# A hybrid decoder layer: three kinds of stores on another queue, rotation tables in two steps, gate weights one unit sooner

## The chip, the cores and the metric

The kernel runs on one core of a Trainium2 chip. A core has a matrix engine (TensorE, PE in the rows; its weight loads are PEld), a vector engine (VectorE, DVE), a scalar engine (ScalarE, ACT), a general one (GpSimd, POOL) and SyncE (SP), which here only starts transfers. Each engine takes its own instructions strictly in order. A transfer (DMA) is started by an instruction on an engine's queue and is then carried out by 16 DMA engines beside the compute; in this kernel nearly all are started from SP, a few from ACT. The metric is the device time of one execution in microseconds, the median of three runs. The granted clock in the rows is 1.00 when TensorE has its full 2.4 GHz and 0.50 at 1.2 GHz; a row between the two is a mean over a stretch.

## The reference

One layer on 2048 tokens of width 1024, all in float32:

```python
h = rmsnorm(x, norm_w)
u, z_s, q, k, v, z_a = split(h @ w_in, 6)            # six blocks of 512 columns
# group A: 32 groups of 16 channels, each a 64-dim complex diagonal state space
xr, xi = associative_scan(a, B u)                      # over 2048 positions
y = gelu(Re(C x) + D * u)
y_s = y * sigmoid(y @ glu_w + glu_b) * silu(z_s)
# group B: 4 heads, two query/key maps of 64, value of 128, causal
q, k = rope(rmsnorm(q)), rope(rmsnorm(k))
w = softmax(q0 k0') - lam * softmax(q1 k1')
y_a = rmsnorm(w @ v) * (1 - lambda_init) * silu(z_a)
x = x + concat(y_s, y_a) @ w_out
gate = sigmoid(x @ ple_w_gate)                         # 1024 x 1024
x = x + gate * (p @ ple_w_proj)                        # p has 256 columns
```

## The kernel before

Every float32 product is made as three passes on TensorE: each operand is split into a high part (a copy rounded to TensorE's float type, made on ACT) and a low part (the rest, made on DVE or POOL by a subtraction), and high x high, high x low and low x high are summed. Intermediate results go to DRAM tensors whose names end in `_scr` and are read back.

**Projections and state space (0 to about 700 us).** The loop at L736 runs over 12 blocks (a half of the tokens, one of the six column blocks), and in each over 4 units of 256 tokens. Eight weight tiles `wraw` of a block are loaded on SP (L279) and split on ACT (L282, `wh`) and DVE (L283, `wl`); a ring of 8 split tiles (`WB`) means that the next block's tiles are made while the last unit of the block runs. Values are scaled on ACT and stored (L831, L832), queries and keys are normalised, rotated, transposed, split and stored as high and low parts (L871, L872). Beside that runs the generator `ssm()` in steps, as background work: for each of 32 channel groups, `ahead` loads the group's input `U` and its rotation table `tab`, TensorE makes two products, DVE rotates by the table, scans and rotates back, and `behind` copies the result to `ysb` on ACT and stores it to `yg_scr` (L652, L653). For every four groups `four` makes what the next four need, in steps of which one is taken per group: it loads parameters, makes `na`, then products and the split `wa`, then two rotation tables `tx` of 128 x 544 on DVE (L581 to L585), each stored to `tab_scr` (L586); `tx` has one buffer, so that the second table is begun when the first one's store has landed. At the end the state-space results pass the half-GLU.

**Attention (about 700 to 1158 us).** Four heads, each over query blocks of 256; the output projection's first half (`pmf`, L928) runs beside it.

**Output projection's second half and the gate (from about 1122 us).** The loop at L1176 takes eight units t = 0 to 7 of 256 tokens. A unit loads `x1` and the attention results, multiplies by `w_out` (L928: in PSUM tile `pmf` for t below 3, `EOP`, in `pm` after that) and adds to `x1` on DVE (L1185, L1189). Between units the gate's weights are prepared: the gate product is made in a way that needs seven combinations of the quarters of `w_gate`, and the generator `gate_w` (L1142) makes their splits in four blocks k = 0 to 3, two steps (`yield`) each. A block loads two 512 KB pieces `wgr` (L1161) in the only two buffers; ahead of each load POOL copies one element of `last[0]`, the `x1` of the unit that was finished one unit earlier, into the buffer (L1160), which holds the load back until that unit's sum is there. ACT makes the high parts (L1149), DVE the differences (L1154) and low parts (L1150), POOL the other low parts (L1150). `GWS` says after which unit how many of the eight steps are written: 2 after t = 3 and t = 4, 3 after t = 5, 1 after t = 6. After the loop `operands` splits the finished `x1` (ACT L1235 `oph`, POOL L1236 `opl`), in memory that the pools of the gate preparation give back, `ple_w` loads the last projection's weights through one buffer `pi` (L1212), and TensorE makes the gate products (L1262) and the last projection (L1278).

**What sets the order.** The program is written in a language with tiles and pools; a scheduler orders each engine's instructions when the program is built, by their priorities (the written order, with background work put behind by `LAG` and attention's scores ahead by `SADV`) and a simulation of its own. A change in one place can thus shuffle instructions elsewhere.

Of the kernel before, what the change touches and what calls it, by code (L numbers as in the profile page):

```python
# [11 lines left out]
F32 = mybir.dt.float32  # L12
# [3 lines left out]
ALU = mybir.AluOpType  # L16
# [49 lines left out]
WB = 8  # L66
ACB = 3
EOP = 3
GWS = {3: 2, 4: 2, 5: 3, 6: 1}
XEB = 14  # L70
RA3 = 2
SSE = 0
# [46 lines left out]
def hymba_kernel(ctx, tc, x_t, p_t, positions, norm_w, w_in, lam_re, lam_im, log_dt, b_re, b_im,  # L119
                 c_re, c_im, ssm_d, glu_w, glu_b, q_norm_w, k_norm_w, lq1, lk1, lq2, lk2,  # L120
                 subln_w, w_out, w_proj, w_gate, out):
    nc = tc.nc
    V, A, G, T = nc.vector, nc.scalar, nc.gpsimd, nc.tensor
# [74 lines left out]
    with ExitStack() as p1:  # L198
# [114 lines left out]
        def ssm():  # L313
# [198 lines left out]
            with tc.tile_pool(name="ssB", bufs=2) as sp:  # L512
# [3 lines left out]
                def split(x_, nm, cols):  # L516

                    hi = sp.tile([128, cols], F32R, name=nm + "h", bufs=SPB[nm])
                    lo = sp.tile([128, cols], F32R, name=nm + "l", bufs=SPB[nm])
                    h_, l_ = hi, lo  # L520
                    if len(x_.shape) > 2:
                        g_, k_, p_ = x_.shape[1:]
                        h_, l_ = (t_.rearrange("q (g l p) -> q g l p", g=g_, l=k_) for t_ in (hi, lo))
                    A.copy(h_, x_)
                    V.tensor_tensor(l_, x_, h_.bitcast(F32), op=ALU.subtract)
                    return hi, lo
# [7 lines left out]
                def spread(par4, o_, l0):  # L534

                    r_ = sp.tile(sh, F32, name="na", bufs=1)
                    t_ = sp.tile([128, 2, 17, 16], F32, name="tabt", bufs=1).rearrange("q s a b -> q (s a b)")[:, :512]
                    t_ = t_.rearrange("q (g l p) -> q g l p", g=4, l=L)
                    V.tensor_tensor(r_, par4[:, :, o_:o_ + 16].unsqueeze(2).to_broadcast(sh),
                                    par4[:, :, 65 + l0:73 + l0].unsqueeze(3).to_broadcast(sh), op=ALU.mult)  # L540
                    V.tensor_tensor(t_, par4[:, :, o_ + 16:o_ + 32].unsqueeze(2).to_broadcast(sh),
                                    par4[:, :, 74 + l0:82 + l0].unsqueeze(3).to_broadcast(sh), op=ALU.mult)
                    V.tensor_tensor(r_, r_, t_, op=ALU.add)
                    return r_

                def four(q4, out_):


                    par4 = sp.tile([128, 4, NPAR], F32, name="parg")
                    nc.sync.dma_start(par4, par_scr[q4])  # L550
                    pt2 = sp.tile([128, 2, NTAB], F32, name="pt2", bufs=1)
                    nc.sync.dma_start(pt2, ptab_scr[q4])
                    na = spread(par4, 0, 1)

                    dd = sp.tile([128, 4, GP], F32, name="dd")
                    nc.sync.dma_start(dd.rearrange("q g p -> q (g p)"), ssm_d[0, q4 * 64:q4 * 64 + 64].partition_broadcast(128))
                    G.affine_select(out=dd, in_=dd, pattern=[[0, 4], [-1, GP]], compare_op=ALU.is_equal,
                                    fill=0.0, base=-112, channel_multiplier=1)
                    yield
                    pr_ = ps_ss.tile([128, 512], F32, name="pss")  # L560
                    for g in range(4):
                        T.matmul(pr_[:, g * 16:g * 16 + 16], lhsT=na[:, g].rearrange("q l p -> q (l p)"),
                                 rhs=par4[:, g, 32:48], start=True, stop=True)
                    rs = sp.tile([128, 64], F32, name="rs", bufs=1)
                    V.tensor_tensor(rs, pr_[:, :64], dd.rearrange("q g p -> q (g p)"), op=ALU.add)
                    nc.sync.dma_start(r_scr[q4][0:128, :], rs)
                    M = sp.tile([128, L, 64], F32, name="M", bufs=1)

                    r0 = r_scr[q4][0:128, :]
                    nc.sync.dma_start(M, bass.AP(tensor=r0.tensor, offset=r0.offset, ap=[[64, 128], [GP * 64, L], [1, 64]]))  # L570
                    pw_ = ps_ss.tile([128, 512], F32, name="pss")
                    for g in range(4):
                        T.transpose(pw_[:, g * 128:g * 128 + 128], na[:, g].rearrange("q l p -> q (l p)"), ident)
                    wa = split(pw_, "wa", 512)
                    yield

                    sht = [128, 2, 17, 16]
                    for e in range(2):
                        tx = sp.tile(sht, F32, name="tx", bufs=1)
                        t1 = sp.tile(sht, F32, name="tabt", bufs=1)  # L580
                        V.tensor_tensor(tx, pt2[:, e, 0:17].unsqueeze(1).unsqueeze(3).to_broadcast(sht),  # L581
                                        pt2[:, e, 34:66].rearrange("q (s b) -> q s b", s=2).unsqueeze(2).to_broadcast(sht), op=ALU.mult)
                        V.tensor_tensor(t1, pt2[:, e, 17:34].unsqueeze(1).unsqueeze(3).to_broadcast(sht),
                                        pt2[:, e, 66:98].rearrange("q (s b) -> q s b", s=2).unsqueeze(2).to_broadcast(sht), op=ALU.mult)
                        V.tensor_tensor(tx, tx, t1, op=ALU.add)  # L585
                        nc.sync.dma_start(tab_scr[q4 * 2 + e], tx)  # L586
                    yield
                    wc = spread(par4, 32, 0)
                    out_[q4] = par4, wa, M, wc
                    yield  # L590
# [21 lines left out]
                for g in range(NG):  # L612
# [35 lines left out]
                    def behind(g=g, py=py, w=[w_[:, gs] for w_ in wc4], xa=xa):  # L648

                        product(py, w, xa, first=False)  # L650
                        ysb = sp.tile([128, NCH], F32, name="ysb", bufs=YSB)
                        A.copy(ysb, py)  # L652
                        nc.sync.dma_start(yg_scr[g].rearrange("l p c -> (l p) c"), ysb)  # L653
                        if g % 8 == 7:
                            for l in range(L):
                                nc.sync.dma_start(
                                    y_scr[(g - 7) * GP:(g + 1) * GP, l, :].rearrange("(g p) c -> g p c", p=GP), yg_scr[g - 7:g + 1, 7 - l])
# [78 lines left out]
        for bi, (hf, kind, c0) in enumerate(blocks):  # L736
            leaving = bi == len(blocks) - 1 or blocks[bi + 1][0] != hf
            for t in range(4):
# [75 lines left out]
                else:  # L814
# [3 lines left out]
                    for j in range(2):  # L818
# [10 lines left out]
                        if kind == "v":  # L829
                            vo = pt.tile([128, 512], F32, name="t2")  # L830
                            A.activation(vo, pm, AF.Copy, scale=rstd[:, ti:ti + 1])  # L831
                            nc.sync.dma_start(v_scr[rows, :], vo)  # L832
                        elif kind == "za":
                            zz = pt.tile([128, 512], F32, name="t2")
                            A.activation(zz, pm, AF.Copy, scale=rstd[:, ti:ti + 1])
# [32 lines left out]
                            V.scalar_tensor_tensor(sl_[dst], ptr, nrm[kind][2], sh_[dst].bitcast(F32), op0=ALU.mult, op1=ALU.subtract)  # L868
                    if kind in ("q", "k"):
                        hi_s, lo_s = (qh_scr, ql_scr) if kind == "q" else (kh_scr, kl_scr)  # L870
                        nc.sync.dma_start(hi_s[:, :, tok:tok + 256].rearrange("h q t -> q h t"), sh_.bitcast(F32))  # L871
                        nc.sync.dma_start(lo_s[:, :, tok:tok + 256].rearrange("h q t -> q h t"), sl_.bitcast(F32))  # L872
                if kind == "u" and (bi, t) != (1, 3):
                    squares(xseq[xi + t])
# [521 lines left out]
```

## Time and profile before

| | us |
|---|---|
| median of three runs | 1471.44 (1465.84 to 1471.6) |
| the profiled execution, whole | 1468.54 |
| its span, first to last instruction | 1466.8 |
| PE busy | 1389.2 (95%) |
| DVE busy | 1067.0 (73%) |
| ACT busy | 768.0 (52%) |
| POOL busy | 522.4 (36%) |

PE is busy or nearly so all along, so the time is the time of TensorE's passes and what it idles. The idle times are read stretch by stretch and by what ended them. A busy PE does not say that it works at its peak, since passes overlap; where the peak matters, the rows below give passes per stretch.

### The profile page before, as it was taken

How to read it: one execution, taken by the hardware profiler on the slowest of the kernel's cores; microseconds unless marked ns; L12 is line 12 of the kernel's file. 1: busy time of each engine (PE TensorE's matmuls, PEld its weight loads, DVE VectorE, ACT ScalarE, POOL GpSimd, SP SyncE). 2: the span in 40 equal slices, each digit the busy share in tenths (PEclk: the TensorE clock that was granted, in tenths of full speed). 3: DMA queues.
4: the chain of work that ended last, by engine and by line, in shares of the span. 5: the costliest groups of instructions: out<-in, count | busy, mean ns of one | idle time of the engine just before them, and what ended most of it. 6: DMA issues, size and time to landing. Idle time of an engine off the chain costs nothing.

```text
span 1466.8 us, 27419 instructions
## 1 busy us (share of the span) xinstructions
PE 1389.2 (95%) x9602; PEld 1279.5 (87%) x9602; DVE 1067.0 (73%) x2527; ACT 768.0 (52%) x1689; POOL 522.4 (36%) x670
## 2 busy tenths in 40 slices
PE   7999899999899999999899999999999996999998
PEld 7998798778698878888699999988989896899998
DVE  8568788789898866774687767767887248656754
ACT  8543335456554545553577677777787213332231
POOL 6632410043010411340255455544335334543440
PEclk9999899999999999999999999999999998899999
DMA  7448666546755287556854644644443455132221
GB/s 244 131 127 263 200 190 210 159 125 211 237 179 177 94 232 185 150 168 203 255 145 125 181 127 119 177 127 152 116 144 122 153 189 205 58 116 76 70 80 58
DMA packets 219410, 230.34 MB, mean 157 GB/s; under 512 B 62712, under 2 KB 168328, under 8 KB 216712
## 3 DMA queue, kind: packets, MB, share of 16 engines
q1 hardware_dynamic: 216968, 224.40, 49.8%
q10 hardware_dynamic: 2304, 4.20, 0.8%
q8 instruction: 75, 1.23, 0.3%
q14 instruction: 63, 0.52, 0.1%
HBM read 152.19 MB, written 84.72 MB: 162 GB/s over the span
## 4 chain that ended last, share of the span: by engine, by line
PE 48%; DVE 19%; DMA 15%; ACT 6%; issue 6%; POOL 5%; SPq 2%; ACTq 0%; DVEq 0%; POOLq 0%
PE pg L1262 11%; PE pmf L928 7%; PE po L1099 7%; PE pss L1063 7%; PE ptw L1095 3%; PE pl L1278 3%; DMA wraw<-in_w_in_dram 3%; PE pmm L824 2%; PE pss L707 2%; PE pmm L778 2%; POOL qst L846 2%; DMA tab_scr<-tx 2%; DVE wl L283 2%; PE pm L928 2%; DVE zz L644 1%
## 5 line engine op out<-in xcount | busy, mean ns | idle before, releaser
L824 PE MATMUL pmm<-wh,xh 128*128 128x512 f32 x512 | 197.6, 395 | 7.0 <-ACT wh L282 6.6
L824 PE MATMUL pmm<-wl,xh 128*128 128x512 f32 x512 | 200.8, 395 | 2.1 <-DVE wl L283 2.1
L824 PE MATMUL pmm<-wh,xl 128*128 128x512 f32 x512 | 200.2, 393 | 0.0
L1063 PE MATMUL pss<-ks,qd 128*128 128x512 f32 (+3 forms) x640 | 185.1, 387 | 7.5 <-DVE st L1065 4.0
L1074 ACT ACTIVATE s<-s,st 128x1024 f32<-128x1024 f32 (+4 forms) x192 | 171.5, 897 | 37.3 <-DVE st L1065 32.8
L1262 PE MATMUL pg<-oph,wg 128*128 128x256 f32 x896 | 164.1, 286 | 15.4 <-ACT oph L1235 15.4
L1262 PEld LDWEIGHTS pg<-oph,wg 128*128 128x128 f32 x896 | 141.6, 195 | 15.6 <-ACT oph L1235 15.6
L1099 PE MATMUL po<-vt,wt 128*128 128x128 f32 x1088 | 152.3, 276 | 2.9 <-ACT yo L1111 1.5
L1099 PEld LDWEIGHTS po<-vt,wt 128*128 128x128 f32 x1088 | 142.2, 192 | 11.2 <-ACT wt L1097 3.2
L1065 DVE CUSTOM_DVE_ANT_0 s<-pss,mk,st 128x512 f32<-128x512 f32 (+2 forms) x192 | 122.1, 651 | 23.3 <-PE pss L1063 21.7
L778 PE MATMUL pmm<-xh,wl 128*128 128x256 f32 x448 | 128.9, 291 | 4.1 <-DVE wl L283 4.1
L778 PE MATMUL pmm<-xh,wh 128*128 128x256 f32 x448 | 124.9, 294 | 6.0 <-DVE stg L788 3.2
L778 PE MATMUL pmm<-xl,wh 128*128 128x256 f32 x448 | 128.5, 290 | 0.0
L1262 PE MATMUL pg<-opl,wg 128*128 128x256 f32 x448 | 127.2, 285 | 0.3 <-POOL opl L1236 0.3
L824 PEld LDWEIGHTS pmm<-wh,xh 128*128 128x128 f32 x512 | 96.2, 189 | 27.6 <-ACT wh L282 8.7
L1063 PEld LDWEIGHTS pss<-ks,qd 128*128 128x128 f32 x640 | 100.8, 192 | 17.5 <-DVE st L1065 8.0
L824 PEld LDWEIGHTS pmm<-wl,xh 128*128 128x128 f32 x512 | 96.6, 189 | 21.1 <-DVE wl L283 3.0
L824 PEld LDWEIGHTS pmm<-wh,xl 128*128 128x128 f32 x512 | 96.7, 189 | 18.2
L928 PE MATMUL pmf<-yh,woh 128*128 128x256 f32 x352 | 105.0, 298 | 4.5 <-DVE x L1185 3.6
L596 POOL TENSOR_TENSOR U<-U,rl 128x256 f32<-128x256 f32 x32 | 28.3, 884 | 220.5 <-DMA U<-ug_scr 169.5
L1065 DVE CUSTOM_DVE_ANT_0 s<-pss,mk 128x512 f32<-128x512 f32 (+3 forms) x128 | 78.5, 629 | 31.2 <-PE pss L1063 26.7
L928 PE MATMUL pmf<-yl,woh 128*128 128x256 f32 x352 | 99.8, 284 | 0.0
(385 smaller groups left out, 3906.1 us busy)
## 6 DMA issues: line engine op xcount, KB each, us to landing
wraw<-in_w_in_dram SPq DMA_DIRECT2D x96, 256.0 KB
xraw<-in_x_t_dram SPq DMA_DIRECT2D x40, 256.0 KB
tab<-tab_scr SPq DMA_DIRECT2D x64, 136.0 KB
qd<-qh_scr SPq DMA_DIRECT2D x64, 128.0 KB
qd<-ql_scr SPq DMA_DIRECT2D x64, 128.0 KB
xr<-in_x_t_dram SPq DMA_DIRECT2D x32, 256.0 KB
yin<-yt_scr SPq DMA_DIRECT2D x16, 512.0 KB
xp_scr<-xp SPq DMA_DIRECT2D x32, 256.0 KB
```

The costliest lines, as they stand in the source:

```text
L283: V.scalar_tensor_tensor(wl, raw, nw[:, k:k + 1], wh.bitcast(F32), op0=ALU.mult, op1=ALU.subtract)
L707: T.matmul(pm[:, e, :], lhsT=a_[:, k, m * 128:m * 128 + 128], rhs=b_[k], start=(k == 0 and n == 0), stop=(k == 3 and n == 2))
L778: T.matmul(pm, lhsT=w[b_][:, cb * 128:cb * 128 + 128], rhs=xt[a_][:, k, :], start=(k == 0 and n == 0), stop=(k == 7 and n == 2))
L824: T.matmul(pm, lhsT=xt[a_][:, k, j * 128:j * 128 + 128], rhs=w[b_], start=(k == 0 and n == 0), stop=(k == 7 and n == 2))
L928: T.matmul(pm[:, e, :], lhsT=w[k][b_][:, ms], rhs=y[a_][:, k, :], start=(k == 0 and n == 0), stop=(k == 3 and n == 2))
L1063: T.matmul(pss[:, :cl], lhsT=qd[:, e, m, tq], rhs=ks[m][:, c0:c0 + cl], start=e == 0, stop=e == 1)
L1065: V.tensor_tensor_reduce(sr[m][pi][:, o:o + cl], pss[:, :cl], mk[:, end - cl:end], scale=1.0, scalar=3.4e38 if ci == 0 else st[:, 2 * ci - ...
L1074: A.activation(sr[m][pi][:, :cl], sr[m][pi][:, :cl], AF.Exp, bias=st[:, ci + m:ci + m + 1], scale=-1.0, accum_out=st[:, 12 + 2 * pi + m:13 ...
L1095: T.transpose(ptw[:, k, :], blocks_[kg + k], ident)
L1099: T.matmul(po[:, 0:128], lhsT=wt[:, k, :], rhs=vt[:, kg + k, :], start=kg + k == 0, stop=kg + k == len(blocks_) - 1)
L1262: T.matmul(banks[mp][:, e], lhsT=wg[n][k][b_][:, m * 128:m * 128 + 128], rhs=x_[a_][:, k], start=k == 0 and q == 0, stop=k == 3 and q == 2)
L1278: T.matmul(banks[mp][:, e], lhsT=wp[k][b_][:, m * 128:m * 128 + 128], rhs=p_[a_][:, k], start=(k == 0 and q == 0), stop=(k == 1 and q == 2))
```

## The change

There are three edits, and nothing else is changed:

1. Three kinds of stores are started from ACT's queue and no longer from SP's: the state-space results `ysb` (32 stores), the values `vo` (16) and the high parts of queries and keys `sh_` (16).
2. The code of a rotation table becomes a function `table(e)`; the first table is written at the end of the second step of `four`, the second one in the third step, where both were before.
3. `GWS` is {2: 2, 3: 2, 4: 2, 5: 2}: two of the eight steps of `gate_w` after each of the units 2, 3, 4 and 5.

```diff
-GWS = {3: 2, 4: 2, 5: 3, 6: 1}
+GWS = {2: 2, 3: 2, 4: 2, 5: 2}
...
                     nc.sync.dma_start(pt2, ptab_scr[q4])
+                    def table(e):
+                        sht = [128, 2, 17, 16]
+                        tx = sp.tile(sht, F32, name="tx", bufs=1)
+                        t1 = sp.tile(sht, F32, name="tabt", bufs=1)
...
+                        V.tensor_tensor(tx, tx, t1, op=ALU.add)
+                        nc.sync.dma_start(tab_scr[q4 * 2 + e], tx)
                     na = spread(par4, 0, 1)
...
                     wa = split(pw_, "wa", 512)
+                    table(0)
                     yield
-                    sht = [128, 2, 17, 16]
-                    for e in range(2):
-                        tx = sp.tile(sht, F32, name="tx", bufs=1)
...
-                        nc.sync.dma_start(tab_scr[q4 * 2 + e], tx)
+                    table(1)
                     yield
...
                         A.copy(ysb, py)
-                        nc.sync.dma_start(yg_scr[g].rearrange("l p c -> (l p) c"), ysb)
+                        nc.scalar.dma_start(yg_scr[g].rearrange("l p c -> (l p) c"), ysb)
...
-                            nc.sync.dma_start(v_scr[rows, :], vo)
+                            nc.scalar.dma_start(v_scr[rows, :], vo)
...
-                        nc.sync.dma_start(hi_s[:, :, tok:tok + 256].rearrange("h q t -> q h t"), sh_.bitcast(F32))
+                        nc.scalar.dma_start(hi_s[:, :, tok:tok + 256].rearrange("h q t -> q h t"), sh_.bitcast(F32))
```

The line numbers of the changed kernel are 3 higher from the second half of `four` on (L1163 for L1160, L1153 for L1150, L918 for L915). What the scheduler makes of it is shown at three places.

POOL, from the first block of the gate weights on, in the kernel before (`x_14915` is unit 2's `x1`, `x_15028` unit 3's, `x_15169` unit 4's):

```order
L1160 COPY wgr<-x_14915 128x1 x2
L915 TENSOR_TENSOR yl<-yin,yh 128x1024
L1150 TENSOR_TENSOR wg_14619<-wgr,wg_14618 128x512
L915 TENSOR_TENSOR yl<-yin,yh 128x1024
L1150 TENSOR_TENSOR wg_14627<-wgr,wg_14626 128x512
L1150 TENSOR_TENSOR wg_14635<-wgr,wg_14634 128x512
L1160 COPY wgr<-x_15028 128x1 x2
L1150 TENSOR_TENSOR wg_14621<-wgr,wg_14620 128x512
L915 TENSOR_TENSOR yl<-yin,yh 128x1024
L1150 TENSOR_TENSOR wg_14629<-wgr,wg_14628 128x512
L1150 TENSOR_TENSOR wg_14637<-wgr,wg_14636 128x512
L1160 COPY wgr<-x_15169 128x1 x2
```

The same in the changed kernel (`x_14802` is unit 1's `x1`, `x_14915` unit 2's, `x_15056` unit 3's):

```order
L1163 COPY wgr<-x_14802 128x1 x2
L918 TENSOR_TENSOR yl<-yin,yh 128x1024
L1153 TENSOR_TENSOR wg_14619<-wgr,wg_14618 128x512
L1153 TENSOR_TENSOR wg_14627<-wgr,wg_14626 128x512
L1153 TENSOR_TENSOR wg_14635<-wgr,wg_14634 128x512
L918 TENSOR_TENSOR yl<-yin,yh 128x1024
L1163 COPY wgr<-x_14915 128x1 x2
L918 TENSOR_TENSOR yl<-yin,yh 128x1024
L1153 TENSOR_TENSOR wg_14621<-wgr,wg_14620 128x512
L918 TENSOR_TENSOR yl<-yin,yh 128x1024
L1153 TENSOR_TENSOR wg_14629<-wgr,wg_14628 128x512
L1153 TENSOR_TENSOR wg_14637<-wgr,wg_14636 128x512
```

Block 0 now hangs on unit 1, and block 1 stands where block 0 stood, behind unit 2, with the same neighbours.

ACT, in the first half's value block of the projections, before (`ysb` is the state-space result, `t_4017` a tile of values, `wh` the high part of a weight tile):

```order
L831 ACTIVATE t_4017<-pmm,rstd 128x512
L634 COPY sw<-zz 64x256
L635 ACTIVATE sw<-zz 64x256
L652 COPY ysb<-pss 128x256
L831 ACTIVATE t_4166<-pmm,rstd 128x512
L282 ACTIVATE wh<-wraw,nw 128x512
L524 CAST xah<-md 128x256
```

and in the changed kernel:

```order
L834 ACTIVATE t_4017<-pmm,rstd 128x512
L637 COPY sw<-pss 64x256
L656 DMA yg_scr<-ysb 128x256
L638 ACTIVATE sw<-pss 64x256
L835 DMA v_scr<-t_4017 128x512
L637 COPY sw<-zz 64x256
L638 ACTIVATE sw<-zz 64x256
L834 ACTIVATE t_4166<-pmm,rstd 128x512
L655 COPY ysb<-pss 128x256
L282 ACTIVATE wh<-wraw,nw 128x512
L835 DMA v_scr<-t_4166 128x512
L656 DMA yg_scr<-ysb 128x256
```

The stores now stand among the casts and copies of ACT; SP's order loses them at the same place.

DVE, where the second pair of rotation tables is made, from the first table's sum to the second one's first product, before:

```order
L585 TENSOR_TENSOR tx<-tx,tabt 128x544
L807 SCALAR_TENSOR_TENSOR t_3094<-t_3094,t_3092 128x512
L637 TENSOR_TENSOR md<-md,sw 128x256
L565 TENSOR_TENSOR rs<-pss,dd 128x64
L583 TENSOR_TENSOR tabt<-pt_2149 128x544
L644 SCALAR_TENSOR_TENSOR zz<-parg,md 128x256
L581 TENSOR_TENSOR tx<-pt_2149 128x544
```

and in the changed kernel:

```order
L562 TENSOR_TENSOR tx<-tx,tabt 128x544
L639 TENSOR_TENSOR sw<-sw,tab 128x256
L525 TENSOR_TENSOR xal<-md,xah 128x256
L577 TENSOR_TENSOR rs<-pss,dd 128x64
L810 SCALAR_TENSOR_TENSOR t_3094<-t_3094,t_3092 128x512
L560 TENSOR_TENSOR tabt<-pt_2149 128x544
L640 TENSOR_TENSOR md<-md,sw 128x256
L558 TENSOR_TENSOR tx<-pt_2149 128x544
```

Between the sum of the first table and the first product of the second stand six instructions now, five before.

## Rows read from the trace of the kernel before

**Rows 1.** The page's first line.

```profile
span 1466.8 us, 27419 instructions
```

**Rows 2.** Busy by stretch: length, PE, PEld, DVE, ACT, POOL, clock, DMA, GB/s.

```profile
90.00:690.00 600.00, 576.54 (x3371) 503.84 (x3370) 482.66 (x1235) 290.97 (x622) 135.61 (x158) 0.99 0.61 183
...
730.00:1150.00 420.00, 411.06 (x3119) 384.00 (x3118) 313.82 (x906) 313.74 (x792) 201.82 (x363) 1.00 0.47 139
1150.00:1235.00 85.00, 81.40 (x665) 79.71 (x663) 44.08 (x59) 18.82 (x31) 31.36 (x31) 1.00 0.52 191
1235.00:1252.00 17.00, 1.97 (x8) 1.85 (x8) 11.97 (x15) 7.80 (x12) 6.54 (x4) 0.62 0.41 154
```

**Rows 3.** Waits of PE from 1150 us on: total us, times, longest.

```profile
PE pg L1262 <- ACT oph L1235: 15.4, 1, 15.4
PE pmf L928 <- DVE x L1185: 3.3, 7, 0.5
```

**Rows 4.** Timeline, PE: start, length, line, operation, tiles, shapes, idle before and releaser.

```profile
1234.39 0.28 PE L928 MATMUL pm<-yl,woh 128*128 128x256 f32 x1
1250.03 2.17 PE L1262 MATMUL pg<-oph,wg 128*128 128x256 f32 x8 [15.36 <-ACT oph L1235]
```

**Rows 5.** Timeline, ACT, the operands' first split and the last projection's first input.

```profile
1248.93 1.99 ACT L1235 CAST oph<-x 128x1024 fp32r<-128x1024 f32 x2 [2.98 <-DVE wg L1150]
...
1265.81 0.62 ACT L1220 CAST ph<-pi 128x512 fp32r<-128x512 f32 x1 [1.84 <-DMA pi<-in_p_t_dram]
```

**Rows 6.** Timeline, DVE: gate weights.

```profile
1201.59 4.59 DVE L1154 TENSOR_TENSOR wgt<-wgr,wgt 128x512 f32<-128x512 f32 x2
...
1234.54 1.28 DVE L1150 TENSOR_TENSOR wg<-wgt,wg 128x512 fp32r<-128x512 f32 x2
...
1247.56 1.28 DVE L1150 TENSOR_TENSOR wg<-wgt,wg 128x512 fp32r<-128x512 f32 x2
```

**Rows 7.** Timeline, POOL: the holds of blocks 0 and 3, the last projection's input.

```profile
1192.84 0.30 POOL L1160 COPY wgr<-x 128x1 f32<-128x1 f32 x2 [5.07 <-DVE x L1185]
...
1233.55 0.63 POOL L1160 COPY wgr<-x 128x1 f32<-128x1 f32 x2 [1.28 <-DVE wgt L1154]
...
1266.51 1.74 POOL L1221 TENSOR_TENSOR pl<-pi,ph 128x512 fp32r<-128x512 f32 x1 [0.49 <-ACT ph L1220]
```

**Rows 8.** Timeline, SP: unit 1's store, block 0's loads, the last projection's first weights.

```profile
1165.28 0.32 SPq L1191 DMA_DIRECT2D x_scr<-x  x1
...
1193.21 1.34 SPq L1161 DMA_DIRECT2D wgr<-in_ple_w_gate_dram  x2
...
1235.47 0.37 SPq L1212 DMA_DIRECT2D pi<-in_ple_w_proj_dram  x1
```

**Rows 9.** The chain that ended last: start, length, what.

```profile
1252.49 23.86 PE pg L1262 x184
1276.35 2.88 PE pl L1278 x24
...
1305.15 23.04 PE pg L1262 x192
```

**Rows 10.** Busy by stretch, around a wait of 4 us in the projections.

```profile
160.00:180.00 20.00, 16.02 (x87) 15.11 (x86) 16.82 (x34) 7.34 (x13) 8.89 (x13) 0.74 0.60 179
```

**Rows 11.** Waits of PE, 90 to 690 us.

```profile
PE pmm L824 <- ACT wh L282: 6.6, 3, 3.5
PE pmm L778 <- DVE wl L283: 4.1, 2, 4.0
PE pmm L824 <- DVE wl L283: 2.1, 2, 1.9
PE pmm L778 <- ACT wh L282: 2.0, 1, 2.0
```

**Rows 12.** Waits of SP's queue, 90 to 690 us.

```profile
SPq L653 <- ACT ysb L652: 18.1, 11, 7.0
```

**Rows 13.** Waits of DVE, 90 to 690 us.

```profile
DVE tx L581 <- DMA tab_scr<-tx: 14.0, 7, 5.8
```

**Rows 14.** The store that ACT starts before: ns min/median/max, first and last start.

```profile
L839 ACTq DMA_DIRECT2D za_scr<-t x16: 326/326/386, 365.1 to 718.0; - x16
```

More of the change, by code (lines that the diff above doesn't have):

```diff
@@ L552, in four @@
                     nc.sync.dma_start(pt2, ptab_scr[q4])
+                    def table(e):
+                        sht = [128, 2, 17, 16]
+                        tx = sp.tile(sht, F32, name="tx", bufs=1)
+                        t1 = sp.tile(sht, F32, name="tabt", bufs=1)
+                        V.tensor_tensor(tx, pt2[:, e, 0:17].unsqueeze(1).unsqueeze(3).to_broadcast(sht),
+                                        pt2[:, e, 34:66].rearrange("q (s b) -> q s b", s=2).unsqueeze(2).to_broadcast(sht), op=ALU.mult)
+                        V.tensor_tensor(t1, pt2[:, e, 17:34].unsqueeze(1).unsqueeze(3).to_broadcast(sht),
+                                        pt2[:, e, 66:98].rearrange("q (s b) -> q s b", s=2).unsqueeze(2).to_broadcast(sht), op=ALU.mult)
+                        V.tensor_tensor(tx, tx, t1, op=ALU.add)
+                        nc.sync.dma_start(tab_scr[q4 * 2 + e], tx)
                     na = spread(par4, 0, 1)
@@ L574, in four @@
                     wa = split(pw_, "wa", 512)
+                    table(0)
                     yield
-                    sht = [128, 2, 17, 16]
-                    for e in range(2):
-                        tx = sp.tile(sht, F32, name="tx", bufs=1)
[L580 to L585, printed above, removed]
-                        nc.sync.dma_start(tab_scr[q4 * 2 + e], tx)
+                    table(1)
                     yield
```

## Prediction

> **What bounds the kernel now.** I read the views in this order: the page's head, busy time by stretch, the waits of PE, the chain, the timelines around the one long wait, and then the waits of SP, DVE and PE in the projections. The span is 1466.8 us [rows 1]; the whole profiled execution is 1468.54 us, so 1.7 us lie outside the span. In the stretches [rows 2] the reader is to see that PE is the bound nearly everywhere and where it is not: it idles 23.5 of 600 us in the projections (600.00 less 576.54), 8.9 of 420 in attention, 3.6 of 85 while the second half of the output projection runs alone, and 15.0 of 17 between that and the gate. The last is one single wait of 15.4 us for `oph` [rows 3, 4], the longest there is, and the third edit reaches it. The first two edits can only touch the 23.5 us of the projections.
>
> **The gate weights.** The path of the wait: PE ends its last pass of the units at 1234.39 + 0.28 = 1234.67 [rows 4]. ACT can cast `oph` only when DVE has made the last low part of block 3 (the releaser named in [rows 5]), since the operands lie in memory that the gate preparation gives back: DVE ends at 1247.56 + 1.28 = 1248.84 [rows 6], ACT starts at 1248.93, PE at 1250.03. The four blocks run one behind the other, since a block needs both `wgr` buffers: POOL's copies that hold the loads back stand at 1192.84 for block 0 and at 1233.55 for block 3 [rows 7], so three blocks take 40.7 us, 13.6 each. Block 0 starts when unit 2's sum is there (POOL waited for DVE's `x`).
>
> In the changed kernel block 0 hangs on unit 1, whose store starts at 1165.28 [rows 8]. With 13.6 us a block it is done at about 1179, well ahead of 1192.84, where block 1 now starts behind unit 2. POOL's order for blocks 1 to 3 has the neighbours that blocks 0 to 2 had before. So block 3 should end where block 2 ended: 1234.54 + 1.28 = 1235.82 [rows 6], 13.0 us before 1248.84. Every instruction moves with it (two loads, seven casts, seven low parts and four differences a block); the units' time on PE does not change. PE then starts the gate at 1250.03 - 13.0 = 1237.0, and 2.3 us of idle time behind 1234.67 remain. **Term: -13.0 us.**
>
> The clock: after the wait the granted clock of the stretch 1235 to 1252 is 0.62 [rows 2], a mean of both levels. The first eight gate passes and the wait for `opl` behind them take 1252.49 - 1250.03 = 2.46 us, and the next 184 take 23.86 [rows 4, 9], where 192 passes at the full clock take 23.04, 0.12 each. So 26.32 us are spent on 23.04 us of work: 3.3 us lost. With 2.3 us of idle time the loss may go or stay. An idle stretch of a few microseconds did cost the clock once: 160 to 180 us has 0.74 [rows 10]. Between 0 and -3.3 I take the middle. **Term: -1.6 us.**
>
> What block 0 collides with: its work now lies beside units 2 and 3, where PE shares one PSUM tile `pmf` with DVE's sums and already waits seven times 0.5 us [rows 3]. DVE is slow when POOL works beside it: two differences took 4.59 us [rows 6], where the low parts take 0.64 each. Unit 2's sums can come some microseconds late; PE has passes of unit 3 between them, which hide most of it. Bounds: 0 (all hidden) to +4.6 (one such pair in full). I take +1, nearer to hidden, since DVE is busy only 44 of 85 us there [rows 2]. **Term: +1 us.**
>
> The last projection's weights become due sooner. They pass one buffer, started from 1235.47 on [rows 8]; the first `ph` is cast at 1265.81 and its low part ends at 1266.51 + 1.74 = 1268.25 [rows 5, 7], 8.1 us ahead of their use at 1276.35 [rows 9]. Use comes 13.0 to 16.3 us sooner, at 1260 to 1263. SP has no other work left before these loads once block 3's are issued 13 us sooner, so they can start up to 12 us sooner, and the first cast and subtraction no longer stand behind block 3's. If half of that comes through, `ph` is just in time. Bounds 0 to +8; I take 0 and keep the rest as a rival.
>
> **The stores.** 64 starts go from SP to ACT. The one kind of store that ACT starts already costs 0.33 us of its queue [rows 14]: 64 x 0.33 = 21 us more on ACT, which is busy 291 of 600 us [rows 2]; that is hidden as long as no cast that PE waits for stands behind. The stores need only what ACT itself has made, so they wait for no other engine's result. On SP go 64 starts and the wait for `ysb`, 18.1 us in eleven pieces [rows 12], behind which weight loads stand. What PE can win is bounded by its waits for split weights: 6.6 + 4.1 + 2.1 + 2.0 = 14.8 us [rows 11], less one of 4.0 in the stretch 160 to 180 us [rows 10], where the state space has not begun to store results. Of the 10.8 left, the weights' own transfer time stays; the starts that leave SP's queue stand ahead of a block's weights two to four at a time, about 1 us. Bounds: -10.8 to +21 (all of ACT's new starts on PE's path). Near the idle shares I take -2. **Term: -2 us.**
>
> The Trainium skill speaks against this edit: the page "DMA: Bandwidth & Descriptors", section "Issuing engines are not separate DMA queues", says that transfers started from different engines end up on the same 16 DMA engines and mix, and that starting from several saves only the sequencer's time. By that rule alone the term would shrink towards 0 and the sum would be 2 us higher; the 18.1 us that SP stands still behind `ysb` is what the rule leaves out, and the trace has it [rows 12].
>
> **The tables.** DVE waits 14.0 us in seven pieces for the first table's store to land before it begins the second [rows 13]. The code separates the two by a step, but the scheduler had spread them before: between the first table's sum and the second's first product stand six instructions where five stood, as the order shows. So this edit hardly does what it says. What may shorten the wait is that stores no longer queue ahead of the table's on SP. **Term: 0**, bounds -2 to +2, within the projections' idle time.
>
> Attention's order is shuffled here and there, with no instruction added; its 8.9 us of idle time are the bound of a gain, and I allow 4 us either way.
>
> **The sum.** 13.0 + 1.6 - 1 + 2 = 15.6 us less: 1468.54 - 15.6 = 1452.9. The profiled execution is 2.9 us under the median of the three runs; I put half of that on top: **1454 us**.
>
> **Rivals.**
> 1. Block 0 does not run sooner: its loads or tiles wait for memory that attention holds, or units 2 and 3 lose on PE what the gate gains. For it: attention ends only shortly before 1165. Against it: the loads need just the copy, which follows unit 1's sum. Only the stores' -2 would be left: 1468.5 - 2, and 1 for the median, 1467 us. Chance 0.09.
> 2. The last projection's weights are late: the buffer's chain starts at 1235 as before, so `ph` is ready at 1268 where PE wants it at 1260, and 8 us of the 13 turn into a new wait. For it: the chain of four loads through one buffer takes 30 us. Against: SP is free sooner. 1454 + 8 = 1462 us. Chance 0.11.
> 3. Slower: ACT becomes the late engine in the projections. It takes instructions in order, so a store that has to wait for its result or a free transfer holds the casts of the next block's weights. ACT idles 309 of 600 us, 4.8 us a store, so the average is covered; it decides against the change once PE sees more than 23 us, 0.36 a store, which is 15.6 given back and 7.4 more. If each start, with an assumed 0.2 us of waiting, is seen in full, 64 x 0.53 = 34 us: 1454 + 2 + 34 = 1490 us. For it: the stores stand next to `wh` in the order. Against: only 8.6 of PE's waits there are for ACT's `wh` [rows 11]. Chance 0.06.
> 4. The projections win more, 10 us, as SP runs ahead: 1446 us. Chance 0.08.
>
> **Chances and range.** The forecast's own case has 0.66, with 1448 to 1460 as its range. A measurement of this kernel tells 0.5%, about 7 us, from no change, so faster is below 1464 us: the forecast, rival 4 and most of rival 2, 0.84. The same: rival 1 and what is left of 2, 0.10. Slower: rival 3, 0.06. The range reaches down past rival 4 and up to rival 1: 1442 to 1467 us.
>
> **What would show it.** In the changed profile: PE's wait for `oph` at about 2 us, block 0's copy on POOL near 1165 less what the projections gained, the first gate passes at 0.12 us each (the clock), no wait of PE at the first L1281 passes, PE's waits for `wh` and `wl` at 12 us or less between 90 and 690, DVE's wait for the tables still over 10 us. I am wrong if the wait for `oph` stays over 8 us, if a wait for `ph` or `wph` appears, or if PE's idle time in the projections grows.

## The result and the profile after

The changed kernel takes 1454.04 us (median of five runs, 1451.45 to 1457.1), the kernel before 1468.45 us on the same chip: ratio 0.9900, 95% interval 0.9875 to 0.9925, so 14.4 us less. The forecast was 1454 us. The profiled execution is 1456.93 us long, 2.9 above that median, with a span of 1455.2 us: 11.6 less than before [rows 1].

Busy by stretch in the changed kernel (columns as in [rows 2]):

```profile
90.00:690.00 600.00, 576.43 (x3377) 501.20 (x3375) 484.23 (x1232) 292.42 (x623) 139.04 (x160) 0.99 0.62 183
...
1150.00:1235.00 85.00, 82.19 (x675) 80.69 (x673) 51.57 (x69) 25.31 (x48) 36.75 (x38) 1.00 0.58 216
1235.00:1252.00 17.00, 13.30 (x88) 12.94 (x89) 10.31 (x9) 4.96 (x7) 9.39 (x3) 0.80 0.15 47
```

Only the last row differs by more than a microsecond of PE: 88 gate passes where 8 stood. The projections, which two of the three edits aim at, have the same 576.4 us. PE's waits from 1150 us on, and PE's timeline at the place:

```profile
PE pg L1265 <- ACT oph L1238: 3.2, 1, 3.2
PE pmf L931 <- DVE x L1188: 2.1, 6, 0.4
PE pg L1265 <- POOL opl L1239: 1.2, 1, 1.2
```

```profile
1234.04 0.28 PE L931 MATMUL pm<-yl,woh 128*128 128x256 f32 x1
1237.54 2.13 PE L1265 MATMUL pg<-oph,wg 128*128 128x256 f32 x8 [3.22 <-ACT oph L1238]
1240.84 0.58 PE L1265 MATMUL pg<-opl,wg 128*128 128x256 f32 x1 [1.16 <-POOL opl L1239]
```

The units end at 1234.32, before at 1234.67 [rows 4]; the wait falls from 15.36 to 3.22; the gate takes 0.9 longer. That is the span's whole difference: -0.35 - 12.14 + 0.9 = -11.6. The chain of waits has the next passes:

```profile
1240.84 23.91 PE pg L1265 x184
1264.74 2.88 PE pl L1281 x24
```

The first 192 gate passes and the wait in them take 3.30 + 23.91 = 27.2 us, before 2.46 + 23.86 = 26.3 [rows 4, 9]. The clock (seventh number of the row) did fall:

```profile
1234.00:1238.00 4.00, 0.78 (x5) 0.61 (x4) 4.00 (x7) 2.08 (x3) 0.47 (x1) 0.95 0.22 66
1238.00:1242.00 4.00, 2.84 (x13) 2.44 (x12) 3.97 (x3) 1.02 (x3) 4.00 (x2) 0.50 0.00 0
1242.00:1246.00 4.00, 4.00 (x27) 4.00 (x26) 2.65 (x1) 0.95 (x1) 4.00 (x2) 0.69 0.05 15
```

What led to the wait, on POOL (the holds of blocks 0 to 3, the last projection's input), on DVE, on ACT and on SP:

```profile
1164.36 0.30 POOL L1163 COPY wgr<-x 128x1 f32<-128x1 f32 x2 [1.32 <-DVE x L1188]
1192.56 0.31 POOL L1163 COPY wgr<-x 128x1 f32<-128x1 f32 x2 [5.14 <-DVE x L1188]
1207.71 1.12 POOL L1163 COPY wgr<-x 128x1 f32<-128x1 f32 x2 [0.68 <-DVE wgt L1157]
1220.79 0.64 POOL L1163 COPY wgr<-x 128x1 f32<-128x1 f32 x2 [0.67 <-POOL wg L1153]
...
1260.38 1.30 POOL L1224 TENSOR_TENSOR pl<-pi,ph 128x512 fp32r<-128x512 f32 x1 [4.57 <-ACT ph L1223]
```

```profile
1234.96 1.28 DVE L1153 TENSOR_TENSOR wg<-wgt,wg 128x512 fp32r<-128x512 f32 x2
1236.16 1.27 DVE L1192 TENSOR_TENSOR x<-x,pm 128x512 f32<-128x512 f32 x2
```

```profile
1236.41 1.99 ACT L1238 CAST oph<-x 128x1024 fp32r<-128x1024 f32 x2 [1.92 <-DVE wg L1153]
...
1259.68 0.62 ACT L1223 CAST ph<-pi 128x512 fp32r<-128x512 f32 x1 [1.27 <-DMA pi<-in_p_t_dram]
```

```profile
1234.35 0.33 SPq L1215 DMA_DIRECT2D pi<-in_ple_w_proj_dram  x1
```

Block 0 begins at 1164.36, block 1 where block 0 began before. Block 3's low parts end at 1236.24. The last two sums of the units stand behind them on DVE and end at 1237.43, the first cast of `oph` ends within 0.02 us of them, and PE starts at 1237.54.

### The profile page after: what moved, and what is told of

It is laid out like the page before. It is cut to its first block, busy times and chain, and to the rows that moved or that the text cites. A ratio compares the mean times of both kernels' runs of the same rounds, so it can differ in the third digit from the quotient of the medians.

```text
span 1455.2 us, 27348 instructions
## 1 busy us (share of the span) xinstructions
PE 1388.3 (95%) x9602; PEld 1275.4 (88%) x9602; DVE 1070.6 (74%) x2527; ACT 768.8 (53%) x1689; POOL 523.3 (36%) x670
## 5 line engine op out<-in xcount | busy, mean ns | idle before, releaser
L1066 PEld LDWEIGHTS pss<-ks,qd 128*128 128x128 f32 x640 | 100.0, 190 | 20.6 <-DVE st L1068 10.4
L827 PEld LDWEIGHTS pmm<-wh,xl 128*128 128x128 f32 x512 | 97.1, 190 | 18.1
L931 PE MATMUL pmf<-yh,wol 128*128 128x256 f32 x352 | 99.7, 283 | 0.0
```

The costliest lines, as they stand in the source:

```text
L827: T.matmul(pm, lhsT=xt[a_][:, k, j * 128:j * 128 + 128], rhs=w[b_], start=(k == 0 and n == 0), stop=(k == 7 and n == 2))
L931: T.matmul(pm[:, e, :], lhsT=w[k][b_][:, ms], rhs=y[a_][:, k, :], start=(k == 0 and n == 0), stop=(k == 3 and n == 2))
L1066: T.matmul(pss[:, :cl], lhsT=qd[:, e, m, tq], rhs=ks[m][:, c0:c0 + cl], start=e == 0, stop=e == 1)
```

## Experiments

Each was timed in five rounds against the kernel before on the same chip. "Wait" is PE's idle time between the units' last pass and the next pass there, "rest" the time from the end of the units' last pass to the end of the span: it leaves out the first 1200 us, which scatter (the projections' last pass ends between 704.4 and 712.7 us in these traces, without order).

| kernel | ratio to before (interval) | us | wait | rest |
|---|---|---|---|---|
| before | 1 | | 15.4 | 232.2 |
| changed | 0.9900 (0.9875 to 0.9925) | -14.4 | 3.2 | 220.9 |
| e1 gate weights alone | 0.9928 (0.9909 to 0.9947) | -10.6 | 3.5 | 221.1 |
| e2 stores alone | 0.9998 (0.9986 to 1.0010) | -0.3 | 15.8 | 232.7 |
| e3 tables alone | 1.0019 (1.0002 to 1.0036) | +2.8 | 16.0 | 232.2 |
| e4 one more unit sooner | 0.9942 (0.9926 to 0.9958) | -8.5 | 1.3 | 219.4 |
| e5 changed again | 0.9902 (0.9888 to 0.9915) | -14.4 | 3.3 | 221.8 |
| e6 gate and stores | 0.9911 (0.9898 to 0.9924) | -13.1 | 3.0 | 221.2 |
| e7 one unit later | 0.9967 (0.9955 to 0.9979) | -4.8 | 11.4 | 228.6 |
| e8 gate and tables | 0.9931 (0.9919 to 0.9942) | -10.1 | 1.8 | 219.9 |
| e9 other hold | 0.9905 (0.9880 to 0.9930) | -13.9 | 1.2 | 219.5 |
| e10 filled | 0.9917 (0.9895 to 0.9940) | -12.2 | 2.6 | 220.7 |
| e11 low part on DVE | 0.9908 (0.9885 to 0.9931) | -13.5 | 2.7 | 219.6 |
| e12 no idle | 0.9887 (0.9864 to 0.9910) | -16.6 | 0 | 215.8 |

**e1, the third edit alone.**

```diff
-GWS = {3: 2, 4: 2, 5: 3, 6: 1}
+GWS = {2: 2, 3: 2, 4: 2, 5: 2}
```

> The kernel before with the third edit alone (GWS {2: 2, 3: 2, 4: 2, 5: 2}). Theory 1 (the whole gain is the shorter wait for oph, stores and tables are worth nothing): 12 to 15 us faster than before, PE's first gate pass 12 to 13 us sooner, PE's wait for oph about 3 us. Theory 2 (the stores give part of the 14.4 us): only 9 to 12 us faster, with the rest showing up in e2. Theory 3 (stores or tables cost a little and hide part of the gate's gain, as the projections' end is 1.1 us later in the changed kernel): over 15 us faster, and the last projection pass earlier than in the changed kernel.

10.6 us faster (7.8 to 13.4), the rest 11.0 us shorter: three quarters of the gain and all but 0.2 us of what the trace shows. Theory 3 is out; theories 1 and 2 both touch the interval. PE waits a little longer for the sums of `pmf` than before (3.3 us [rows 3]):

```profile
PE pmf L928 <- DVE x L1185: 3.9, 8, 0.6
```

**e2, the stores alone.**

```diff
-nc.sync.dma_start(yg_scr[g].rearrange("l p c -> (l p) c"), ysb)
+nc.scalar.dma_start(yg_scr[g].rearrange("l p c -> (l p) c"), ysb)
...
-nc.sync.dma_start(v_scr[rows, :], vo)
+nc.scalar.dma_start(v_scr[rows, :], vo)
...
-nc.sync.dma_start(hi_s[:, :, tok:tok + 256].rearrange("h q t -> q h t"), sh_.bitcast(F32))
+nc.scalar.dma_start(hi_s[:, :, tok:tok + 256].rearrange("h q t -> q h t"), sh_.bitcast(F32))
```

> The kernel before with the 64 stores on ACT's queue alone. Theory 1: within 2 us of before, PE busy and idle in 90 to 690 us as before, while SP's wait for ysb is gone and other waits of SP have grown by as much. Theory 2: 2 to 5 us faster, PE's idle time in 90 to 690 us below 22 us. Theory 3: 1 to 4 us slower, with casts of weights late on ACT.

No difference, to 2 us. Two waits of SP from 90 to 690 us, before and in e2, then the stretch in e2:

```profile
SPq L599 <- DVE md L637: 13.9, 8, 3.4
SPq L279 <- DVE wl L283: 20.6, 24, 4.0
```

```profile
SPq L599 <- DVE md L637: 27.3, 11, 5.3
SPq L279 <- DVE wl L283: 27.1, 26, 9.9
```

```profile
90.00:690.00 600.00, 575.24 (x3367) 502.59 (x3365) 481.51 (x1232) 291.88 (x622) 139.70 (x158) 0.99 0.61 182
```

The 18.1 us behind `ysb` [rows 12] are gone, and the same queue now stands longer behind DVE's results. PE is busy 575.2 us, before 576.5 [rows 2]. Its waits for split weights did fall, from 14.8 us [rows 11] to 7.0:

```profile
PE pmm L824 <- ACT wh L282: 3.2, 2, 1.8
PE pmm L778 <- DVE wl L283: 2.3, 3, 1.6
PE pmm L824 <- DVE wl L283: 1.5, 2, 0.8
```

In the five kernels with these stores on SP they are 10.4 to 14.8 us, in the nine with them on ACT 6.1 to 10.4. But PE's waits of all kinds in the stretch add up to 24.3 us, before 22.9: others grew instead, for `wal` from 1.8 to 3.3, for `xah` from 0.2 to 2.1, and for the loads of `ks` from nothing to 2.1. So the weights came sooner and the projections gained nothing by it. The Trainium skill's rule (page "DMA: Bandwidth & Descriptors", section "Issuing engines are not separate DMA queues": starting from several engines saves only sequencer time) agrees with this run, whose ratio is 0.9998.

**e3, the tables alone.**

```diff
                     wa = split(pw_, "wa", 512)
+                    table(0)
                     yield
...
+                    table(1)
                     yield
```

> The kernel before with the table function in two steps alone. Theory 1: within 2 us of before, since between the two tables on DVE the scheduler leaves about as many instructions as before, and DVE's wait for the first table's store stays above 10 us. Theory 2: 2 us or more faster, with that wait below 5 us. Theory 3: 1 to 2 us slower.

2.8 us slower, with an interval that just leaves out zero; beside the gate weights (e8 against e1) it is 0.5. No gain in either. Where the 2.8 us arise is open: the rest is that of before. DVE's wait is what it was [rows 13]:

```profile
DVE tx L558 <- DMA tab_scr<-tx: 14.2, 6, 5.8
```

**e4, one more unit sooner.**

```diff
-GWS = {2: 2, 3: 2, 4: 2, 5: 2}
+GWS = {1: 2, 2: 2, 3: 2, 4: 2}
```

> The changed kernel with the gate weights one unit sooner again (GWS {1: 2, 2: 2, 3: 2, 4: 2}). Theory 1: nothing of the 13 us repeats, since in the changed kernel only 3.2 us of the wait for oph are left and part of that is the last unit's own sum and the cast itself (1.0 us for one): 1 to 3 us faster than the changed kernel, 14 to 17 us faster than before, and the granted clock behind the wait still falls. Rival a (the fall of the clock hangs on these 3 us): the gate's first 192 passes take 23.0 to 23.5 us in place of 27.2, and it is 4 to 6 us faster than the changed kernel. Rival b (the units lose by the work beside them, or memory that the attention holds keeps block 0 back): the same as the changed kernel or slower, with the unit's passes ending later than 1234.3.

5.9 us behind the changed kernel by the ratios: rival b. The wait has shrunk, but blocks 0 and 1 lie beside the passes that go through `pmf`, and PE waits for those sums longer than in the changed kernel (2.1 us), in one piece 1.9:

```profile
PE pmf L931 <- DVE x L1188: 5.5, 7, 1.9
PE pg L1265 <- ACT oph L1238: 1.5, 2, 1.3
PE pg L1265 <- POOL opl L1239: 1.2, 1, 1.2
```

The units' last pass ends at 1237.56, 3.2 us later, though the projections ended 3.6 us sooner. The longer waits for the sums are 3.4 of these 6.8 us; where the others arise is not shown.

**e5, e6 and e8, the changed kernel again and two pairs.** e5 is the changed kernel as it is. e6 has the edits of e1 and e2, e8 those of e1 and e3; against the changed kernel, e6 takes back the tables, and e8 the stores:

```diff
-                    table(0)
                     yield
-                    table(1)
+                    for e in range(2):
+                        tx = sp.tile(sht, F32, name="tx", bufs=1)
...
```

```diff
-nc.scalar.dma_start(yg_scr[g].rearrange("l p c -> (l p) c"), ysb)
+nc.sync.dma_start(yg_scr[g].rearrange("l p c -> (l p) c"), ysb)
... (the same for `vo` and `sh_`)
```

> The changed kernel once more, on the chip of the next three. The edits alone gave 10.6 (gate), 0.3 (stores) and -2.8 us (tables), 8.1 together; the changed kernel gave 14.4, with an interval of 3.7 either way. Theory 1 (the edits simply add, the rest is scatter between executions, which spread over 9 us in before): 8 to 12 us faster than before now. Rival (the edits help one another by 3 to 6 us): 13 to 16 us faster again.

> Gate weights one unit sooner and the stores on ACT's queue, tables as before. Theory 1: 9 to 13 us faster than before, the same as the gate edit alone. Rival (stores and tables only help together, since stores gone from SP let the second table begin sooner): the same as the gate edit alone, and 3 to 5 us behind the changed kernel. Rival (the stores cost nothing only while the tables lie badly): over 13 us faster.

> Gate weights one unit sooner and the tables in two steps, stores on SP's queue as before. Theory 1 (edits add): 6 to 12 us faster than before. Rival (the tables alone do cost 2.8 us): 7 to 9 us faster and slower than the kernel with gate and stores. Rival (tables gain once the gate is sooner): over 13 us faster.

The 14.4 us come again (12.5 to 16.4), so the edits do not simply add: 10.6 + 0.3 - 2.8 = 8.1 (4 to 12 by the three intervals together). With the gate weights sooner, the stores seem to bring something: the changed kernel is 0.9902/0.9931 of e8, 4.3 us less (the two intervals together leave 1.7 to 6.9); e6 against e1 gives 2.5, within scatter. It can't lie behind the units, since e8's rest is 0.9 us shorter than the changed kernel's, and ahead of them the traces scatter and show no wait that accounts for it. This stays open.

**e7, one unit later.**

```diff
-GWS = {3: 2, 4: 2, 5: 3, 6: 1}
+GWS = {4: 2, 5: 2, 6: 3, 7: 1}
```

> The kernel before with the gate weights one unit later (GWS {4: 2, 5: 2, 6: 3, 7: 1}). Theory 1 (a link of the chain of the four blocks is worth its 13 us wherever PE waits for the last one): 12 to 15 us slower than before, PE's wait for oph 27 to 30 us, and no further loss by the clock (the gate's first 192 passes take 26 to 27.5 us as before). Rival a (the units themselves are cheaper without a block beside them, so that part comes back): 8 to 11 us slower. Rival b (blocks that lie beside nothing run faster than 13.6 us): 6 to 10 us slower, with blocks 2 and 3 under 11 us each.

It is faster than before by 4.8 us, and all three expectations fall. POOL's holds of blocks 0 and 1:

```profile
1179.37 0.30 POOL L1160 COPY wgr<-x 128x1 f32<-128x1 f32 x2 [16.84 <-DVE x L1189]
1197.54 0.30 POOL L1160 COPY wgr<-x 128x1 f32<-128x1 f32 x2 [3.67 <-issue]
```

Block 0 now hangs on unit 3, written later, and yet it starts 1228.98 - 1179.37 = 49.6 us ahead of the units' end, before 1234.67 - 1192.84 = 41.8 [rows 4, 7]. In before, unit 3's last sum on DVE is this row:

```profile
1184.31 0.69 DVE L1189 TENSOR_TENSOR x<-x,pm 128x512 f32<-128x512 f32 x1 [1.50 <-PE pm L928]
```

Unit 3 was complete at 1185.0 and unit 2, whose passes go through the one tile `pmf`, at 1192.8. The units are not finished in the order in which they are written: the kernel before had its first block held by the later of the two.

**e9, the other hold.** If that is so, block 1 of the changed kernel, which unit 2 holds until 1192.56, can start sooner behind unit 3.

```diff
-GWS = {2: 2, 3: 2, 4: 2, 5: 2}
+GWS = {2: 2, 4: 4, 5: 2}
```

> The changed kernel with GWS {2: 2, 4: 4, 5: 2}: block 1 is held by unit 3's sum in place of unit 2's, block 2 by unit 3's, block 3 by unit 4's. New theory (in before and in the changed kernel one hold, unit 2's sum at 1192.6 to 1192.8, which ends after unit 3's since its passes go through the one tile pmf, sets the blocks behind it; beyond that hold the blocks follow one another by their buffers): block 1's copy on POOL about 8 us sooner against the end of the units' passes than in the changed kernel (41.8 us ahead of it there), PE's wait for oph 1.3 us as with the gate weights two units sooner, no fall of the units, 1 to 3 us faster than the changed kernel, 14 to 17 us faster than before. Rival (unit 2's late sums are DVE's, and a block beside them makes them later): PE's waits for pmf's sums grow from 2 to over 5 us, and it is the same as the changed kernel or slower.

```profile
1161.59 0.30 POOL L1163 COPY wgr<-x 128x1 f32<-128x1 f32 x2 [1.32 <-DVE x L1188]
1181.86 0.30 POOL L1163 COPY wgr<-x 128x1 f32<-128x1 f32 x2 [7.09 <-DVE x L1192]
1197.03 1.12 POOL L1163 COPY wgr<-x 128x1 f32<-128x1 f32 x2 [0.68 <-DVE wgt L1157]
1209.06 0.63 POOL L1163 COPY wgr<-x 128x1 f32<-128x1 f32 x2 [1.29 <-DVE wgt L1157]
```

```profile
1221.25 1.88 DVE L1153 TENSOR_TENSOR wg<-wgt,wg 128x512 fp32r<-128x512 f32 x3
```

```profile
1231.48 1.99 ACT L1238 CAST oph<-x 128x1024 fp32r<-128x1024 f32 x2 [10.09 <-PE pm L931]
```

Block 1 starts 49.5 us ahead of the units' end (1231.39), 7.8 more than in the changed kernel, and blocks 2 and 3 follow when the buffers come free. Block 3's low parts end at 1223.13, 8.3 us ahead of the units' end, so the blocks no longer decide anything. What is left of the wait, 1.2 us, is the first cast of `oph`, which starts 0.1 us behind the units' last pass and takes 1.05; block 3 could be sooner still and nothing would be won. The rest is 1.4 us shorter, as expected; the times can't tell so little.

**e10, filled.** 24 passes that nobody reads, written ahead of the gate into a `pg` tile.

```diff
+idle = ps_g.tile([128, 2, 256], F32, name="pg3")
+for _ in range(24):
+    T.matmul(idle[:, 0], lhsT=wg[7][3][0][:, 0:128], rhs=wg[7][3][0][:, 0:256], ...)
 def product(n, x_):
```

> The changed kernel with 24 passes of 128 x 256 on the last block's high part added between the units and the gate, into a tile that nobody reads (work that the reference doesn't have). They take 2.9 us at the full clock, in the wait of 3.2 us for oph. Theory (the clock falls because PE idles there): the granted clock stays at 1.00 from 1234 to 1255 us, the gate's first 192 passes and the wait for opl take 24 to 25.5 us in place of 27.2, 2 to 3 us faster than the changed kernel. Rival a (the wait for opl, which grows to 2 us at the full clock, makes it fall all the same): same clock rows as the changed kernel, later by 1 to 2 us, and the same time. Rival b (the fall doesn't hang on idle time): clock at 0.5 for 7 us beside busy passes.

```profile
1238.29 4.60 PE L1260 MATMUL pg<-wg 128*128 128x256 f32 x24 [2.64 <-ACT oph L1238]
1242.72 0.88 PE L1269 MATMUL pg<-oph,wg 128*128 128x256 f32 x6
```

```profile
1234.00:1238.00 4.00, 1.65 (x14) 1.45 (x13) 4.00 (x7) 2.07 (x3) 0.00 (x0) 1.00 0.20 66
1238.00:1242.00 4.00, 3.71 (x19) 3.75 (x20) 3.97 (x3) 1.67 (x3) 3.72 (x2) 0.58 0.00 0
1242.00:1246.00 4.00, 4.00 (x35) 4.00 (x35) 3.45 (x2) 1.05 (x1) 4.00 (x2) 1.00 0.00 0
```

The fill did not go into the wait, though it does not read `oph`. Its tile comes from the pool that follows the one of the units' sums in PSUM, and the last of those sums ended at 1238.18 on DVE, within 0.02 us of the first cast of `oph`. So the wait that the trace puts down to `oph` probably ends by those sums too; one trace can't tell the two apart, but in e12 the same passes into one of the units' own tiles start at once. The clock fell all the same, so this run does not test the theory. What it shows: 24 added passes made the rest no longer (220.7, changed 220.9). They ran while the clock was low and the low part was being made, and the 192 real passes behind them took 23.04 us, the full clock.

**e11, the first low part on DVE.**

```diff
-yield made(xi_[:, K1])
+yield made(xi_[:, K1], V if xi_ is kept[0] else G)
```

> The changed kernel with the first operand's low part made on DVE in place of POOL. In the changed kernel the two low parts take POOL 6.6 us (4.7 in before) beside DVE's two differences, and PE waits 1.2 us for the first. Theory: PE's wait for opl below 0.5 us, 1 us faster than the changed kernel, which the times can't tell from no change. Rival: DVE's part comes behind its difference, and the wait stays or turns into one for the second low part.

The wait for `opl` falls from 1.16 to 0.09 us and the rest is 1.2 us shorter, as expected, below what the times tell.

**e12, no idle.** e9 and e11 together, and 12 passes behind the units into one of the units' own PSUM tiles.

```diff
+idle = ps3.tile([128, 2, 256], F32, name="pm3")
+for _ in range(12):
+    T.matmul(idle[:, 0], lhsT=wg[7][3][0][:, 0:128], rhs=wg[7][3][0][:, 0:256], ...)
```

> The other hold (GWS {2: 2, 4: 4, 5: 2}), the first operand's low part on DVE, and 12 passes on the last block's high part written behind the units, into one of the units' own PSUM tiles, so that they need not wait for the last sums (work that the reference doesn't have; 1.4 us at the full clock, where 1.2 us of wait are left). From the end of the units' last pass to the end of the span the changed kernel took 220.9 us, with the other hold 219.5. Theory (idle time of PE is what makes the clock fall): no wait over 0.5 us from 1200 us on, the granted clock stays at 1.00, that time is 215 to 217 us, 18 to 20 us faster than before and 3 to 5 us faster than the changed kernel. Rival a (the clock falls at this place whatever PE does, as it did beside passes without a gap in the filled kernel once they had begun): the clock is at 0.5 for some 6 us of passes all the same, 218.5 to 219.5 us, 14 to 16 us faster than before. Rival b (the 0.2 to 0.5 us that remain suffice): the same rows as rival a, but with the fall just behind such a gap.

```profile
1231.53 0.28 PE L931 MATMUL pm<-yl,woh 128*128 128x256 f32 x1
1231.64 1.59 PE L1202 MATMUL pm<-wg 128*128 128x256 f32 x12
1233.34 1.33 PE L1268 MATMUL pg<-oph,wg 128*128 128x256 f32 x8
1234.86 0.38 PE L1268 MATMUL pg<-opl,wg 128*128 128x256 f32 x1 [0.19 <-DVE opl L1242]
```

```profile
1230.00:1234.00 4.00, 3.90 (x33) 3.63 (x31) 2.16 (x3) 2.00 (x2) 0.00 (x0) 1.00 0.18 66
1234.00:1238.00 4.00, 3.81 (x31) 3.61 (x31) 4.00 (x2) 0.62 (x1) 3.04 (x1) 1.00 0.00 0
```

The clock stays at 1.00 and the rest is 215.8 us, within the 215 to 217 of the theory: 5.0 less than in the changed kernel, 1.7 of it the shorter time to the first gate pass (1.5 us, was 3.2) and 3.3 the clock and the wait for `opl`. The kernel is 16.6 us faster than before (13.2 to 19.9), an interval that holds the theory's 18 to 20 and rival a's 14 to 16; it is the clock and the rest that decide for the theory. The passes and the low part on DVE were not tried apart on top of e9. Against the changed kernel the stretch is shorter in the trace, but the intervals of the ratios overlap: that it is faster as a whole is likely, not shown.

## Why the prediction was right, and where it was wrong

**Gate weights, -13.0: right.** The first gate pass comes 12.5 us sooner and the wait is 12.1 shorter. The step "block 3 should end where block 2 ended" held to 0.4 us (1236.24 for 1235.82). The wait is 3.2 us in place of 2.3: 0.4 by block 3's later end, 0.35 since the units ended sooner, 0.1 between the low parts and PE. The prediction had block 1 begin where block 0 had begun, behind unit 2, and so it was (1192.56), 12 us after block 0 was done. What it did not see is that this hold is the lever: unit 3 is complete before unit 2, so that a block written later can begin sooner (e7, e9). And the hold matters only up to the units' end: in e9 block 3 is done 8.3 us ahead of it, and 1.2 us of wait are left.

**Clock, -1.6: wrong.** It became +0.9. "Between 0 and -3.3 I take the middle" put a loss at half that comes whole or not at all in these runs. "With 2.3 us of idle time the loss may go or stay": it stayed whole, and the wait for `opl` grew from 0.3 to 1.2 us, since POOL's two low parts run beside DVE's differences (6.57 us, before 4.72). e4 and e9, with 1.2 us of wait and 1.2 behind it, lost the clock too; of these kernels only e12, without a wait over 0.2 us, kept it.

**Block 0 beside units 2 and 3, +1: about right.** In e1, with the gate weights alone, PE's waits for the sums went from 3.3 to 3.9 us and the units ended 0.2 us later. The 2.1 us of the changed kernel are no gain: of its waits for `pmf` one of 1.9 us lies ahead of 1150 us. Counted from 700 us on they are 3.6 before, 4.1 in e1, 3.7 in e2 and 4.0 in the changed kernel, so block 0 cost about half a microsecond. The danger was real one unit further on (e4).

**The last projection's weights, 0: right for another reason.** "They can start up to 12 us sooner" was wrong: the first one started at 1234.35, before at 1235.47 [rows 8]. It does not wait for block 3's loads, which were issued by 1221.8, but starts 0.03 us behind the units' last pass, and so it is in every run here in which the gate's last loads were issued 3 us or more ahead of that. But the input's cast came 25.3 us behind it, before 30.3, and its low part was ready at 1261.68, 3.1 us ahead of its use. Rival 2 missed by those 3 us.

**Stores, -2: alone nothing** (-2.1 to +1.5), with the gate weights 2.5 or 4.3, open as said. The step that took SP's wait of 18.1 us for a cost was wrong: it turned into other waits of SP, and where the weights did come sooner, PE waited for other results instead (e2). Rival 3 fell: the stores alone cost at most 1.5 us.

**Tables, 0: right beside the gate weights** (+0.5), and too good for the tables alone (+2.8, 0.3 to 5.3), where the bound was +2.

**The sum.** The profiled execution gave -11.6 for -15.6: of the 4.0 us between them 0.9 is the gate's wait, 2.5 the clock and 2 the stores, less 1.4 for the units. The median gave -14.4; its last 3 us have no place in the profiled execution, which lies at the upper end of its kernel's runs. They came again in e5, and no term of the prediction and no wait of the traces stands for them. The 1.5 us on top, put there for a median of 1471.44, were not needed either: beside the changed kernel the kernel before took 1468.45. So the hit at 1454 rests on the gate weights; that it is so close is luck.

**The signs.** Most came true: block 0's copy at 1164.36, no wait for `ph`, PE's waits for `wh` and `wl` 6.1 us, DVE's for the tables 10.4. The wait for `oph` is 3.2 us where about 2 stood, and the one for the clock failed: the first gate passes did not take 0.12 us each.

## What to carry to other kernels

Before moving a preparation sooner, look up which result holds it, and when that result is there: units that share one PSUM tile may be complete after units that were written later. When TensorE's wait shrinks but does not vanish, count its clock as lost until a trace shows otherwise: here from 3.2 to 1.2 us of wait gave 1.4 us (e9), what was left of it and the wait for `opl` gave 3.7 (e12). A wait on a queue is a cost only if something on the path stands behind it, and taking it away is first seen in which wait follows.

## What was not expected of the hardware

In e9 PE waited 1.18, 0.21 and 1.26 us between the units' last pass and the ninth gate pass, and the clock fell to 0.50 (1.2 GHz) within the third of these waits; in e12, where 12 passes filled the first and the low part on DVE left 0.2 us of the third, it stayed at 1.00. Beside each other, DVE and POOL lose in turn: in the changed kernel a DVE difference of 128 x 1024 took 3.26 us and POOL's pair of low parts 6.57; in e11 two DVE operations of that size took 1.22 each there, and POOL's one low part 5.15, where the shortest in these traces take 2.4.
